# Sums of weight blocks in one ring with all other pieces, and one fixed PSUM tile for the product banks

## The chip, the cores and the metric

The kernel runs on one core of a Trainium2 chip. The metric is device time in microseconds. The kernel before took 2430.69 us, the median of three runs (2430.39 to 2430.94).

## What is computed

A trunk of two layers over 256 positions of width 2048, all in float32. Layer 0 mixes positions with a bidirectional mLSTM of 8 heads, layer 1 with a bidirectional HGRN2 of 16 heads; after each mixer comes a gated MLP of inner width 5504 with a convolution of width 3. Cut to the parts that the change touches, which are the matrix products with large weights:

```python
h = h + mixer(rmsnorm(h, g), w_in, ...) @ w_out          # w_out 2048 x 2048

u = rmsnorm(h, g2) @ w_up                                # w_up 2048 x 11008
a, v = jnp.split(u, 2, axis=-1)
c = conv_b + sum(ap[:, j:j + s] * conv_w[j] for j in range(3))
h = h + (jax.nn.gelu(c, approximate=False) * v) @ w_down # w_down 5504 x 2048
...
return rmsnorm(h, final_g)
```

## The kernel before

*Products in three matmuls.* TensorE multiplies in a float32 form of reduced precision, so every weight block and every activation is split in two parts, high and low (`wh`, `wl`; `xh`, `xl`), and a product is xh wh + xh wl + xl wh. ScalarE makes the high part (a cast), VectorE the low part (a subtraction). Weights pass through this once each: SP loads them in pieces of up to 1 MB into `raw` (three places), and `parts` splits them 1024 columns at a time into `wh` and `wl`, four places each.

*Chunks.* The kernel is a list of chunks, run one after the other by `stream`: "fm" (outputs by feature, the up-projection, q, k and gates), "tm" (outputs by token) and "st". `stream` takes split pieces from the generator `split_weights`, `LOOK` = 3 pieces ahead of their use. Every other job (norms, heads, sums of activations, the preparation below) is a generator in `side`, advanced by `tick`.

*The st chunks* are pairs of output columns computed by `squares_by_seven`. The 256 positions are two halves of 128, a pair of output blocks is two of 512 columns, and the inner dimension goes in units of two blocks of 128 rows. A plain unit needs eight products. Units named in `SEVEN` (for the MLP) or `SEVEN_MIX` (for the mixers' output) are done in seven, in Winograd's manner, with sums of activation blocks S1 to S4 and sums of weight blocks T1 to T4. A unit's weights lie in memory as B11, B22, B21, B12. The products P1, P5, P6, P7 collect in four PSUM banks of the pool `psm` (tag `mm`, two places of two banks, also used by the fm and tm chunks in turn), C11 to C22 in the four banks of `psa`. When the last unit by seven is done, `mid` reads P1, P5, P6, P7 into the output; after the last unit `done` adds C11 to C22.

In the MLP each part of the inner dimension (22 blocks, then 21) first runs its up-projection chunks. During these, `prepare` forms T1 to T4 of the coming units and writes them to memory (`tscr`). The first part then has two st chunks (d0 and d1, 11 units each, eight of them by seven), the second part has one st chunk (d0, 11 units, six by seven) and two tm chunks. In the mixers' output product there is one st chunk of 8 units, three by seven, whose T1 to T4 `weight_sums` forms on the spot.

*Where sums of weights live.* For a unit by seven, `combine` (L199 to L211) loads T1 to T4 as two tiles `T` of 1024 columns (tag `avc`, three places in the MLP, shared with the up-projection's evacuations `avc` of `done_up`, L1132 to L1143; two places in the mixers) or forms them, and splits them (L208, L209) into `th0`, `tl0`, `th1`, `tl1`, of which there is one place each. This is done for unit u+1 before unit u's first piece is split, or with `late` (mixers) after it. The two pieces of weights of unit u go through `wh`, `wl`; the sums are handed over with the second.

*Order.* Each engine runs its instructions in an order that was fixed at build time from a simulated timeline: an instruction goes in when its inputs and a place for its output are there, the ones that stand earlier in the program first. `pin` and `late(dst, src)` keep program order.

Of the kernel before, what the change touches and what calls it, by code (L numbers as in the profile page):

```python
# [8 lines left out]
F32 = mybir.dt.float32  # L9
# [33 lines left out]
RAW = 3  # L43
WB = 4
MIX = 5
LEAD = 48
TEMP = 3
GATES = 4 * AH
SEVEN = (1, 2, 3, 5, 6, 7, 8, 9), (1, 2, 4, 5, 7, 8)
SCRATCH = 4096  # L50
# [9 lines left out]
def trunk_kernel(ctx, tc, xT, x_d, fg_d, pp_d, cst_d, w_gate, w_first, w_aq, w_ak, w_av, w_ao, w_aout, w_ao2,  # L60
# [6 lines left out]
    ev = ctx.enter_context(tc.tile_pool(name="ev", bufs=1))  # L67
    psm = ctx.enter_context(tc.tile_pool(name="psm", bufs=2, space=PSUM))
    psa = ctx.enter_context(tc.tile_pool(name="psa", bufs=4, space=PSUM))
# [53 lines left out]

    pin = tc.keep_in_program_order

    def load_raw(src, b0, b1, start=nc.sync.dma_start):
# [4 lines left out]
    def split_weights(chunks):  # L131

        def parts(r, m, pin=lambda ins: ins):
            wh = wpool.tile([P, 1024], F32R, tag="wh", bufs=WB, name="wh")
            wl = wpool.tile([P, 1024], F32R, tag="wl", bufs=WB, name="wl")
            pin(act.copy(wh[:, :m], r))  # L136
            pin(dve.tensor_tensor(wl[:, :m], r, wh[:, :m].bitcast(F32), ALU.subtract))  # L137
            return wh, wl

        first, loaded = chunks[0], []  # L140
        raws = first.load(loaded, chunks[1])
        for k in range(KT):
            if k == 0:
                first.x(0, pin)
            wh, wl = parts(raws[k], 512, pin)
            if k:
                first.x(k, pin)
            yield wh, wl, 1
        for ch in chunks[1:]:
            if ch.kind == "st":  # L150
                yield from split_squares(ch, parts)
                continue
            total = ch.nk * ch.width
            for b0 in range(0, total, 2048):
                b1 = min(total, b0 + 2048)
                raw = loaded.pop(0) if loaded else load_raw(ch.src, b0, b1, late if ch.paced else nc.sync.dma_start)
                for c0 in range(0, b1 - b0, 1024):
                    m = min(1024, b1 - b0 - c0)
                    at = b0 + c0 if ch is chunks[1] else total
                    if at == 0:  # L160
                        first.gate()
                    if at < LOOK * 1024:
                        wh, wl = parts(raw[:, c0:c0 + m], m, pin)
                    elif ch is chunks[2] and b0 == c0 == 0:
                        wh, wl = parts(raw[:, c0:c0 + m], m, first.behind_v)
                    else:
                        wh, wl = parts(raw[:, c0:c0 + m], m)
                    if at == (LOOK - 1) * 1024:
                        first.sums()
                    yield wh, wl, m // ch.width  # L170

    def temporary(pool_, name):
        return pool_.tile([P, 1024], F32, tag="avc", bufs=TEMP if pool_.name == "ff" else 2, name=name)

    def weight_sums(a, b, T, T_):

        B22, B21, B12 = a[:, 512:1024], b[:, 0:512], b[:, 512:1024]
        dve.tensor_tensor(T.rearrange("p (a b) -> p a b", a=2), B12.unsqueeze(1).broadcast_to([P, 2, 512]),
                          a.rearrange("p (a b) -> p a b", a=2), ALU.subtract)
        yield 2.5  # L180
        dve.tensor_tensor(T_[:, 0:512], B22, T[:, 0:512], ALU.subtract)
        yield 2.5
        dve.tensor_tensor(T_[:, 512:1024], B21, T_[:, 0:512], ALU.subtract)

    def split_squares(ch, parts):

        units, raws, kept, sums = (ch.nk + 1) // 2, {}, {}, {}
        side.until(lambda: ch.waits is None or ch.waits)

        def raw(u):  # L190
            if u not in raws and u < units:
                raws[u] = load_raw(ch.src, 2048 * u, min(2048 * (u + 1), 1024 * ch.nk) - (512 if u in ch.stored else 0))
                if u in ch.stored:
                    kept[u] = [temporary(ch.pool, "T") for _ in range(2)]
                    for i, t in enumerate(kept[u]):
                        nc.sync.dma_start(t, ch.stored[u][:, i * 1024:(i + 1) * 1024])
            return raws.get(u)

        def combine(u):  # L199
            r = raw(u)  # L200
            T, T_ = kept[u] if u in kept else (temporary(ch.pool, "T") for _ in range(2))
            if u not in kept:
                for _ in weight_sums(r[:, 0:1024], r[:, 1024:2048], T, T_):
                    pass
            sums[u] = []
            for i, t in enumerate((T, T_)):
                th, tl = (ch.pool.tile([P, 1024], F32R, tag=n, name=n) for n in (f"th{i}", f"tl{i}"))
                act.copy(th, t)  # L208
                dve.tensor_tensor(tl, t, th.bitcast(F32), ALU.subtract)  # L209
                sums[u].append((th, tl))  # L210

        for u in range(units):
            r = raw(u)
            if u + 1 in ch.seven and not ch.late:
                combine(u + 1)
            wh, wl = parts(r[:, 0:1024], 1024)
            yield wh, wl, 1
            if u + 1 in ch.seven and ch.late:
                combine(u + 1)
            if 2 * u + 1 < ch.nk:  # L220
                m = 512 if u in ch.seven else 1024
                wh, wl = parts(r[:, 1024:1024 + m], m)
                yield wh, wl, sums.pop(u, None)

    def banks():
        return psm.tile([P, 2, 512], F32, tag="mm", name="mm")

    def squares_by_seven(ch, fetch, ready):
# [19 lines left out]
        for u in range(units):  # L248
# [3 lines left out]
            if 2 * u + 1 == ch.nk:  # L252
# [4 lines left out]
                break  # L257
            fetch()
            q = ready.pop(0)
            x0, x1 = ch.x(2 * u), ch.x(2 * u + 1)  # L260
            A11, A21, A12, A22 = half(x0, 0), half(x0, 1), half(x1, 0), half(x1, 1)
            B11, B22, B21 = block(p[:2], 0), block(p[:2], 1), block(q[:2], 0)
            if u in ch.seven:
                (S1, S3, S2, S4), t = ch.sums(u), q[2]
                T1, T3, T2, T4 = (block(t[i // 2], i % 2) for i in ((3, 1, 0, 2) if u in ch.stored else range(4)))
                for i, (ps, x, w) in enumerate(((P1, A11, B11), (C12, S4, B22), (C11, A12, B21), (P5, S1, T1),
                                                (P7, S3, T3), (P6, S2, T2), (C21, A22, T4))):
                    product(ps, x, w, u == last and ps in psm_)
                    side.tick(0.65)
                if u == last:  # L270
                    ch.mid(psm_)
                continue
            B12 = block(q[:2], 1)
            for ps, (x, w), (y, v) in ((C11, (A11, B11), (A12, B21)), (C12, (A11, B12), (A12, B22)),
# [78 lines left out]

    def fm_sum(ps, dst):
        b = ev.tile([P, T], F32, tag="b", bufs=3, name="b")
        act.copy(b, ps[:, T:2 * T])
        dve.tensor_tensor(dst, ps[:, 0:T], b, ALU.add)

    def fm_scaled(ps, R, dst, scale=None):
        fm_sum(ps, dst)  # L360
        if scale is None:
# [179 lines left out]

    def pair(src, nk, c0, x, sums, norm, seven, late=False):

# [29 lines left out]
        ch = Chunk("st", src, nk, x, done)  # L573
        ch.mid, ch.seven, ch.sums, ch.late = mid, seven, sums, late
        ch.stored, ch.waits = {}, None
        return ch

    def prepare(mp, todo, period, finished):
# [3 lines left out]
        def load(i):  # L582
            if i < len(todo):
                n = ("th", "tl")[i % 2]
                r = [mp.tile([P, 1024], F32, tag=f"{n}{j}", name=f"p{n}") for j in range(2)]
                for j in range(2):
# [16 lines left out]
    def mixed(w, w2, x, norm, close):  # L603
# [7 lines left out]

        two = pair(w2, KT, 1, x, sums, norm, SEVEN_MIX, True)

# [21 lines left out]
    def mlstm(norm, nxt):  # L635
# [114 lines left out]
        def two_parts(ps, name, scale=None):  # L750
            z = box["mp"].tile([P, T], F32, tag="qk", bufs=2, name="qk")
            zs = box["mp"].tile([P, 2 * T], F32R, tag=name, bufs=2, name=name)
            fm_scaled(ps, norm.R, z, scale)
            act.copy(zs[:, 0:T], z)
# [73 lines left out]
        for pr in range(AH // 2):  # L828
# [36 lines left out]
            def done_first(ps, done_v=done_v):  # L865
                pq = aux("pq")
                for k in range(KT):
                    o = k % 4 * GATES
                    pin(pe.matmul(pq[o:o + GATES, 0:T], gw[:, k], hx[:, k], start=k < 4, stop=k >= KT - 4))
                gs = ev.tile([P, T], F32, tag="b", bufs=3, name="gs")  # L870
                act.copy(gs, pq[:, 0:T])
# [40 lines left out]
    def hgrn(norm, nxt):  # L912
# [33 lines left out]
        def take(hd, what, ps):  # L946
            mp = box["mp"]
            st = heads[hd]
            if what == 0:
                st["q"] = mp.tile([P, T], F32, tag="q", bufs=2, name="q")  # L950
                fm_scaled(ps, norm.R, st["q"], box["oml"][:, hd:hd + 1])
                st["QK"] = mp.tile([P, 1152], F32, tag="QK", bufs=2, name="QK")
# [5 lines left out]
            z = mp.tile([P, T], F32, tag="z", bufs=2, name="z")  # L958
            fm_scaled(ps, norm.R, z)
            g = G[:, dr * T:(dr + 1) * T]  # L960
# [352 lines left out]
```

## Time and profile before

| | us, unless named |
|---|---|
| median of three runs | 2430.69 |
| the profiled execution | 2427.93 |
| its span | 2426.2 |
| moved by DMA | 578.14 MB, mean 238 GB/s |

The core's TensorE clock was 0.997 of full speed over the span. "PE" is TensorE's matmuls, "PEld" its weight loads, which overlap them; "DVE" is VectorE, "ACT" ScalarE, "POOL" GpSimd, "SP" the queue that issues nearly all loads. L238 is line 238 of the kernel, the matmul in `product` of `squares_by_seven`. A row of a stretch names its start and end in us from the span's start, its length, each engine's busy time with its count, the granted TensorE clock, the mean busy share of the 16 DMA engines and GB/s. A row of waits reads: engine, what it was about to do, what it waited for, us in total, times, longest. A row of a group reads: line, engine, operation, output and inputs, shapes, count, then busy us, mean ns of one, then the idle time before them and what ended it. The matmuls are pipelined, so that one shows 0.39 us though the next starts 0.23 us after it.

### The profile page before, as it was taken

To read this page: it belongs to the slowest core of one execution; us is meant where nothing else is said; L and a number is where in the kernel's file an instruction comes from. 1 tells how busy PE (TensorE), PEld (TensorE's weight loads), DVE (VectorE), ACT (ScalarE), POOL (GpSimd) and SP (SyncE) were. 2 spreads that over 40 slices of the span, in tenths; PEclk is the share of its full clock that TensorE was granted. 3 is DMA by queue.
4 is the path that set the end of the run, shared out by engine and by line. 5 is a ranking of instruction groups with operands and counts; after the bars stand their busy time and mean duration, and the time that the engine had idled before them with its cause. 6 is when DMAs were issued, how large, how long until landed. Compare 5 with 4: busy or idle time off the path is not lost.

```text
span 2426.2 us, 38067 instructions
## 1 busy us (share of the span) xinstructions
PE 2386.3 (98%) x14596; PEld 2030.4 (84%) x14596; DVE 1933.8 (80%) x3075; ACT 1349.0 (56%) x2055; POOL 194.2 (8%) x240
## 2 busy tenths in 40 slices
PE   9999999999999999999999999999999999999998
PEld 8888888888777888888888888887888877888886
DVE  7766687888778888777888888889798877888875
ACT  7655455555555555555555555556555555455553
POOL 0100000000000000001222232220000000000000
PEclk9999999999999999999999999999999999999999
DMA  8655556998887777755545554545898988777774
GB/s 308 188 180 174 174 191 231 332 332 308 318 305 265 270 241 243 267 193 192 175 159 172 167 172 167 173 158 191 282 340 325 329 305 301 246 250 243 249 269 147
DMA packets 105701, 578.14 MB, mean 238 GB/s; under 512 B 11936, under 2 KB 12448, under 8 KB 58672
## 3 DMA queue, kind: packets, MB, share of 16 engines
q1 hardware_dynamic: 103824, 571.71, 67.4%
q0 software_dynamic: 1120, 3.21, 0.8%
q8 instruction: 114, 1.87, 0.3%
q10 hardware_dynamic: 576, 0.79, 0.1%
q14 instruction: 67, 0.55, 0.1%
HBM read 527.37 MB, written 48.30 MB: 237 GB/s over the span
## 4 chain that ended last, share of the span: by engine, by line
PE 83%; DMA 7%; DVE 6%; issue 2%; ACT 1%; SPq 0%; POOL 0%; POOLq 0%; ACTq 0%; DVEq 0%
PE mm L329 31%; PE mm L345 21%; PE mm L333 16%; PE pc L238 7%; PE mm L238 4%; DVE wl L137 2%; DMA T<-tscr 2%; DMA pth<-in_w_d 2%; DMA ptl<-in_w_d 1%; DVE tl L209 1%; ACT th L208 1%; PE pn L792 1%; DMA raw<-in_w_d 1%; PE py L1050 1%; PE pd L1000 1%
## 5 line engine op out<-in xcount | busy, mean ns | idle before, releaser
L329 PE MATMUL mm<-xt,wh 128*128 128x512 f32 x3776 | 1315.0, 395 | 0.0
L137 DVE TENSOR_TENSOR wl<-raw,wh 128x1024 fp32r<-128x1024 f32 (+1 forms) x846 | 1005.6, 1196 | 303.9 <-ACT wh L136 302.5
L136 ACT CAST wh<-raw 128x1024 fp32r<-128x1024 f32 (+1 forms) x846 | 850.3, 1014 | 675.2 <-PE mm L329 403.8
L333 PE MATMUL mm<-xt,wl 128*128 128x256 f32 x3776 | 1049.2, 279 | 0.4 <-DVE wl L137 0.4
L329 PEld LDWEIGHTS mm<-xt,wh 128*128 128x128 f32 x3776 | 707.7, 188 | 160.3
L333 PEld LDWEIGHTS mm<-xt,wl 128*128 128x128 f32 x3776 | 711.0, 188 | 5.0 <-DVE wl L137 0.8
L345 PE MATMUL mm<-wh,xt 128*128 128x512 f32 x1024 | 322.7, 391 | 1.1 <-ACT xt L351 1.0
L345 PEld LDWEIGHTS mm<-wh,xt 128*128 128x128 f32 x1024 | 191.6, 188 | 40.8 <-ACT xt L351 1.5
L345 PE MATMUL mm<-wl,xt 128*128 128x512 f32 x512 | 200.2, 391 | 0.0
L209 DVE TENSOR_TENSOR tl<-T,th 128x1024 fp32r<-128x1024 f32 x100 | 120.1, 1221 | 60.8 <-ACT th L208 60.5
L238 PE MATMUL pc<-wh,g 128*128 128x512 f32 x488 | 163.3, 391 | 3.4 <-ACT wh L136 3.3
L208 ACT CAST th<-T 128x1024 fp32r<-128x1024 f32 x100 | 102.8, 1050 | 98.1 <-PE mm L238 56.3
L238 PE MATMUL mm<-th,sx 128*128 128x512 f32 x300 | 107.9, 397 | 10.6 <-ACT th L208 10.3
L238 PEld LDWEIGHTS pc<-wh,g 128*128 128x128 f32 x488 | 91.9, 188 | 24.1 <-ACT wh L136 5.1
L345 PEld LDWEIGHTS mm<-wl,xt 128*128 128x128 f32 x512 | 96.2, 188 | 18.9
L558 POOL TENSOR_TENSOR hm<-hm,u 128x512 f32<-128x512 f32 x8 | 12.4, 1546 | 1180.4 <-DVE u L557 1125.2
L345 PE MATMUL mm<-wh,g 128*128 128x512 f32 x308 | 96.3, 391 | 0.0
L238 PE MATMUL pc<-wl,g 128*128 128x512 f32 x244 | 95.6, 392 | 0.1
L1136 ACT ACTIVATE avc<-avc,pp 128x256 f32<-128x256 f32 x86 | 51.7, 601 | 51.4 <-DVE avc L1134 51.0
L238 PEld LDWEIGHTS mm<-th,sx 128*128 128x128 f32 x300 | 56.9, 190 | 26.3 <-ACT th L208 14.3
L597 DVE TENSOR_TENSOR ptl<-ptl 128x512 f32<-128x512 f32 x88 | 60.4, 686 | 23.2 <-DMA ptl<-in_w_d 22.9
L597 DVE TENSOR_TENSOR pth<-pth 128x512 f32<-128x512 f32 x88 | 60.3, 685 | 21.2 <-DMA pth<-in_w_d 15.0
(268 smaller groups left out, 2564.5 us busy)
## 6 DMA issues: line engine op xcount, KB each, us to landing
raw<-in_w_up SPq DMA_DIRECT2D x172, 1024.0 KB, 6.3
raw<-in_w_bq SPq DMA_DIRECT2D x48, 1024.0 KB, 5.0
T<-tscr SPq DMA_DIRECT2D x88, 512.0 KB, 5.5
raw<-in_w_d SPq DMA_DIRECT2D x40, 1024.0 KB, 5.2
raw<-in_w_d SPq DMA_DIRECT2D x44, 768.0 KB, 6.1
raw<-in_w_ao SPq DMA_DIRECT2D x24, 1024.0 KB, 4.8
pth<-in_w_d SPq DMA_DIRECT2D x44, 512.0 KB, 8.0
ptl<-in_w_d SPq DMA_DIRECT2D x44, 512.0 KB, 7.8
```

What stands on the lines that cost most here:

```text
L136: pin(act.copy(wh[:, :m], r))
L137: pin(dve.tensor_tensor(wl[:, :m], r, wh[:, :m].bitcast(F32), ALU.subtract))
L208: act.copy(th, t)
L209: dve.tensor_tensor(tl, t, th.bitcast(F32), ALU.subtract)
L238: pe.matmul(ps, a, b, start=id(ps) not in begun, stop=stop and i == 2)
L329: pe.matmul(ps[f], wh[:, c:c + P], x, start=k + kk == 0, stop=False)
L333: pe.matmul(ps[f][:, 0:T], wl[:, c:c + P], x[:, 0:T], start=False, stop=k + kk == ch.nk - 1)
L345: pe.matmul(ps[t], x[:, a + t * P:a + (t + 1) * P], w[:, c], start=st and i == 0, stop=sp and i == 2)
L597: dve.tensor_tensor(out, x, y, ALU.subtract)
L792: pe.matmul(pn[:, 0:258], w, v, start=(i == 0), stop=(i == len(parts) - 1))
L1000: pe.matmul(pd[o:o + QUAD, c:c + n], k[:, b * QUAD:(b + 1) * QUAD], q[:, t:t + n], start=True, stop=True)
L1136: act.activation(c, a, AF.Identity, bias=col("conv_b", layer * FT + f), scale=cw[1])
```

## The change

- `T` becomes one tile of 1536 columns that holds T2, T3, T4; T1 takes B12's place in `raw`. For stored units that is a load of 768 KB into `T` and one of 256 KB into the last quarter of `raw`, in place of two of 512 KB.
- `th` and `tl` go. A unit by seven now gives four pieces to `parts`: (B11, B22), (T2, T3), (B21, T1), (T4), each in order of use. In st chunks every third piece takes its place in the stage's own pool (tags `wh`, `wl` with `MORE` = 2 places) and the others in `wpool`'s four, so that there are six places in turn.
- For stored units `raw` and `T` are loaded when the unit itself comes; unit u+1 is no longer asked for ahead of unit u. For the mixers `combine` forms the sums of unit u+1 after the first piece of unit u, in four operations of 512 columns.
- The products are run in the order P1, C12, P6, P7, C11, P5, C21 (before: P1, C12, C11, P5, P7, P6, C21).
- The units by seven of the first part are 1 to 4 and 6 to 9 (before: 1 to 3 and 5 to 9).
- The four product banks are one tile, made once, whose halves `banks` hands out in turn.
- `prepare` uses the tags `wh`, `wl` of the stage's pool in place of `th`, `tl`. The buffer `b` of `fm_sum` moves from `ev` to the mixers' pools, and `gs` gets a place of its own.

```diff
-SEVEN = (1, 2, 3, 5, 6, 7, 8, 9), (1, 2, 4, 5, 7, 8)
+MORE = 2
+SEVEN = (1, 2, 3, 4, 6, 7, 8, 9), (1, 2, 4, 5, 7, 8)
...
+    four, turns = psm.tile([P, 4, 512], F32, name="mm"), dict(mm=0, w=0)
...
-        def parts(r, m, pin=lambda ins: ins):
-            wh = wpool.tile([P, 1024], F32R, tag="wh", bufs=WB, name="wh")
-            wl = wpool.tile([P, 1024], F32R, tag="wl", bufs=WB, name="wl")
+        def parts(r, m, pin=lambda ins: ins, more=None):
+            where, bufs = wpool, WB
+            if more is not None:
+                turns["w"] += 1
+                if turns["w"] % 3 == 0:
+                    where, bufs = more, MORE
+            wh, wl = (where.tile([P, 1024], F32R, tag=n, bufs=bufs, name=n) for n in ("wh", "wl"))
...
-        return pool_.tile([P, 1024], F32, tag="avc", bufs=TEMP if pool_.name == "ff" else 2, name=name)
+        return pool_.tile([P, 1536], F32, tag="avc", bufs=TEMP if pool_.name == "ff" else 2, name=name)
...
         def raw(u):
             if u not in raws and u < units:
-                raws[u] = load_raw(ch.src, 2048 * u, min(2048 * (u + 1), 1024 * ch.nk) - (512 if u in ch.stored else 0))
+                n = 1536 if u in ch.stored else min(2048, 1024 * ch.nk - 2048 * u)
+                raws[u] = load_raw(ch.src, 2048 * u, 2048 * u + n)
                 if u in ch.stored:
-                    kept[u] = [temporary(ch.pool, "T") for _ in range(2)]
-                    for i, t in enumerate(kept[u]):
-                        nc.sync.dma_start(t, ch.stored[u][:, i * 1024:(i + 1) * 1024])
+                    kept[u] = temporary(ch.pool, "T")
+                    nc.sync.dma_start(kept[u], ch.stored[u][:, 0:1536])
+                    nc.sync.dma_start(raws[u][:, 1536:2048], ch.stored[u][:, 1536:2048])
             return raws.get(u)
...
         def combine(u):
-            r = raw(u)
-            T, T_ = kept[u] if u in kept else (temporary(ch.pool, "T") for _ in range(2))
-            if u not in kept:
-                for _ in weight_sums(r[:, 0:1024], r[:, 1024:2048], T, T_):
-                    pass
-            sums[u] = []
-            for i, t in enumerate((T, T_)):
-                th, tl = (ch.pool.tile([P, 1024], F32R, tag=n, name=n) for n in (f"th{i}", f"tl{i}"))
-                act.copy(th, t)
-                dve.tensor_tensor(tl, t, th.bitcast(F32), ALU.subtract)
-                sums[u].append((th, tl))
+            r, T = raw(u), temporary(ch.pool, "T")
+            B11, B22, B21, B12 = (r[:, j * 512:(j + 1) * 512] for j in range(4))
+            T2, T3, T4 = (T[:, j * 512:(j + 1) * 512] for j in range(3))
+            for x, y, out in ((B12, B22, T3), (B12, B11, B12), (B22, B12, T2), (B21, T2, T4)):
+                dve.tensor_tensor(out, x, y, ALU.subtract)
+            kept[u] = T
...
         for u in range(units):
             r = raw(u)
-            if u + 1 in ch.seven and not ch.late:
+            yield *parts(r[:, 0:1024], 1024, more=ch.pool), 1
+            if u + 1 in ch.seven and u + 1 not in ch.stored:
                 combine(u + 1)
-            wh, wl = parts(r[:, 0:1024], 1024)
-            yield wh, wl, 1
-            if u + 1 in ch.seven and ch.late:
-                combine(u + 1)
+            if u in ch.seven:
+                yield *parts(kept[u][:, 0:1024], 1024, more=ch.pool), 1
             if 2 * u + 1 < ch.nk:
-                m = 512 if u in ch.seven else 1024
-                wh, wl = parts(r[:, 1024:1024 + m], m)
-                yield wh, wl, sums.pop(u, None)
+                yield *parts(r[:, 1024:2048], 1024, more=ch.pool), 1
+            if u in ch.seven:
+                yield *parts(kept[u][:, 1024:1536], 512, more=ch.pool), 1
...
     def banks():
-        return psm.tile([P, 2, 512], F32, tag="mm", name="mm")
+        turns["mm"] = 2 - turns["mm"]
+        return four[:, turns["mm"]:turns["mm"] + 2]
...
+            def products(*them):
+                for ps, x, w in them:
                     product(ps, x, w, u == last and ps in psm_)
                     side.tick(0.65)
+
+            def piece():
+                fetch()
+                q = ready.pop(0)[:2]
+                return block(q, 0), block(q, 1)
+
+            B11, B22 = block(p[:2], 0), block(p[:2], 1)
             if u in ch.seven:
-                (S1, S3, S2, S4), t = ch.sums(u), q[2]
-                T1, T3, T2, T4 = (block(t[i // 2], i % 2) for i in ((3, 1, 0, 2) if u in ch.stored else range(4)))
-                for i, (ps, x, w) in enumerate(((P1, A11, B11), (C12, S4, B22), (C11, A12, B21), (P5, S1, T1),
-                                                (P7, S3, T3), (P6, S2, T2), (C21, A22, T4))):
-                    product(ps, x, w, u == last and ps in psm_)
-                    side.tick(0.65)
+                S1, S3, S2, S4 = ch.sums(u)
+                products((P1, A11, B11), (C12, S4, B22))
+                T2, T3 = piece()
+                products((P6, S2, T2), (P7, S3, T3))
+                B21, T1 = piece()
+                products((C11, A12, B21), (P5, S1, T1))
+                T4, _ = piece()
+                products((C21, A22, T4))
                 if u == last:
                     ch.mid(psm_)
                 continue
...
-    def fm_sum(ps, dst):
-        b = ev.tile([P, T], F32, tag="b", bufs=3, name="b")
+    def fm_sum(mp, ps, dst):
+        b = mp.tile([P, T], F32, tag="b", bufs=3, name="b")
...
-                n = ("th", "tl")[i % 2]
-                r = [mp.tile([P, 1024], F32, tag=f"{n}{j}", name=f"p{n}") for j in range(2)]
+                n = ("wh", "wl")[i % 2]
+                r = [mp.tile([P, 1024], F32, tag=n, bufs=MORE, name=f"p{n}") for _ in range(2)]
...
-                gs = ev.tile([P, T], F32, tag="b", bufs=3, name="gs")
+                gs = ev.tile([P, T], F32, tag="gs", name="gs")
```

More of the change, by code (lines that the diff above doesn't have):

```diff
@@ L67, in trunk_kernel @@
     ev = ctx.enter_context(tc.tile_pool(name="ev", bufs=1))
-    psm = ctx.enter_context(tc.tile_pool(name="psm", bufs=2, space=PSUM))
+    psm = ctx.enter_context(tc.tile_pool(name="psm", bufs=1, space=PSUM))
     psa = ctx.enter_context(tc.tile_pool(name="psa", bufs=4, space=PSUM))
@@ L172, in temporary @@
     def temporary(pool_, name):
-        return pool_.tile([P, 1024], F32, tag="avc", bufs=TEMP if pool_.name == "ff" else 2, name=name)
[L175 to L183, printed above, removed]
+        return pool_.tile([P, 1536], F32, tag="avc", bufs=TEMP if pool_.name == "ff" else 2, name=name)
     def split_squares(ch, parts):
-        units, raws, kept, sums = (ch.nk + 1) // 2, {}, {}, {}
+        units, raws, kept = (ch.nk + 1) // 2, {}, {}
         side.until(lambda: ch.waits is None or ch.waits)
@@ L257, in squares_by_seven @@
                 break
-            fetch()
-            q = ready.pop(0)
             x0, x1 = ch.x(2 * u), ch.x(2 * u + 1)
             A11, A21, A12, A22 = half(x0, 0), half(x0, 1), half(x1, 0), half(x1, 1)
-            B11, B22, B21 = block(p[:2], 0), block(p[:2], 1), block(q[:2], 0)
-            if u in ch.seven:
-                (S1, S3, S2, S4), t = ch.sums(u), q[2]
-                T1, T3, T2, T4 = (block(t[i // 2], i % 2) for i in ((3, 1, 0, 2) if u in ch.stored else range(4)))
-                for i, (ps, x, w) in enumerate(((P1, A11, B11), (C12, S4, B22), (C11, A12, B21), (P5, S1, T1),
-                                                (P7, S3, T3), (P6, S2, T2), (C21, A22, T4))):
+            def products(*them):
+                for ps, x, w in them:
                     product(ps, x, w, u == last and ps in psm_)
                     side.tick(0.65)
+            def piece():
[3 more added lines that the diff above has]
+            B11, B22 = block(p[:2], 0), block(p[:2], 1)
+            if u in ch.seven:
+                S1, S3, S2, S4 = ch.sums(u)
[6 more added lines that the diff above has]
+                products((C21, A22, T4))
                 if u == last:
@@ L272, in squares_by_seven @@
                 continue
-            B12 = block(q[:2], 1)
+            B21, B12 = piece()
             for ps, (x, w), (y, v) in ((C11, (A11, B11), (A12, B21)), (C12, (A11, B12), (A12, B22)),
@@ L352, in split, with fm_scaled @@
         pin(dve.scalar_tensor_tensor(dst[:, T:2 * T], src, gcol, dst[:, 0:T].bitcast(F32), ALU.mult, ALU.subtract))
-    def fm_sum(ps, dst):
-        b = ev.tile([P, T], F32, tag="b", bufs=3, name="b")
+    def fm_sum(mp, ps, dst):
+        b = mp.tile([P, T], F32, tag="b", bufs=3, name="b")
         act.copy(b, ps[:, T:2 * T])
         dve.tensor_tensor(dst, ps[:, 0:T], b, ALU.add)
-    def fm_scaled(ps, R, dst, scale=None):
-        fm_sum(ps, dst)
+    def fm_scaled(mp, ps, R, dst, scale=None):
+        fm_sum(mp, ps, dst)
         if scale is None:
@@ L540, in token_sums, with pair @@
         return [(sx[:, i * P:(i + 1) * P], sx[:, m + i * P:m + (i + 1) * P]) for i in range(m // P)] + ([last] if last else [])
-    def pair(src, nk, c0, x, sums, norm, seven, late=False):
+    def pair(src, nk, c0, x, sums, norm, seven):
         def part(t, c):
@@ L573, in pair @@
         ch = Chunk("st", src, nk, x, done)
-        ch.mid, ch.seven, ch.sums, ch.late = mid, seven, sums, late
-        ch.stored, ch.waits = {}, None
+        ch.mid, ch.seven, ch.sums = mid, seven, sums
+        ch.stored, ch.waits, ch.pool = {}, None, None
         return ch
@@ L610, in sums @@
             return SX[u]
-        two = pair(w2, KT, 1, x, sums, norm, SEVEN_MIX, True)
+        two = pair(w2, KT, 1, x, sums, norm, SEVEN_MIX)
         def token():
@@ L752, in two_parts @@
             zs = box["mp"].tile([P, 2 * T], F32R, tag=name, bufs=2, name=name)
-            fm_scaled(ps, norm.R, z, scale)
+            fm_scaled(box["mp"], ps, norm.R, z, scale)
             act.copy(zs[:, 0:T], z)
@@ L950, in take @@
                 st["q"] = mp.tile([P, T], F32, tag="q", bufs=2, name="q")
-                fm_scaled(ps, norm.R, st["q"], box["oml"][:, hd:hd + 1])
+                fm_scaled(mp, ps, norm.R, st["q"], box["oml"][:, hd:hd + 1])
                 st["QK"] = mp.tile([P, 1152], F32, tag="QK", bufs=2, name="QK")
@@ L958, in take @@
             z = mp.tile([P, T], F32, tag="z", bufs=2, name="z")
-            fm_scaled(ps, norm.R, z)
+            fm_scaled(mp, ps, norm.R, z)
             g = G[:, dr * T:(dr + 1) * T]
```

## The prediction

> **What bounds the kernel now.** I read the page first, then the busy time of stretches, then who waits for whom inside them.
>
> ```profile
> span 2426.2 us, 38067 instructions
> PE 2386.3 (98%) x14596; PEld 2030.4 (84%) x14596; DVE 1933.8 (80%) x3075; ACT 1349.0 (56%) x2055; POOL 194.2 (8%) x240
> ```
>
> TensorE is busy 98% of the span, so nothing that leaves its matmuls as they are can save much more than its idle 40 us and what it loses in pace. The change touches only the stretches of line 238, the products of `squares_by_seven`. Their matmuls by stretch (us, PE busy and count, PEld, clock, DMA share, GB/s):
>
> ```profile
> 636.50:762.00 125.50, 116.41 (x480) 89.73 (x480) 0.99 0.83 298
> 994.80:1048.00 53.20, 53.19 (x234) 43.77 (x234) 1.00 0.75 269
> 1947.50:2073.50 126.00, 115.28 (x480) 89.99 (x480) 0.99 0.82 293
> 2306.40:2359.60 53.20, 53.20 (x234) 43.73 (x234) 1.00 0.76 275
> ```
>
> The second row gives TensorE's pace when nothing holds it: 53.2 / 234 = 0.2273 us per matmul; the fourth runs at the same. The first and third are the double pairs at the first part of each FFN (d0 and d1, 22 blocks of rows each, 480 matmuls): 480 x 0.2273 = 109.1 us, so they lose 16.4 and 16.9 us. The last stretch with line 238 is the middle of the second mixer's output product; here all engines' rows (PE, PEld, DVE, ACT, POOL) are needed:
>
> ```profile
> 1630.70:1677.20 46.50, 44.52 (x192) 34.93 (x190) 41.07 (x60) 24.52 (x31) 0.00 (x0) 1.00 0.50 173
> 323.90:365.40 41.50, 41.50 (x185) 34.37 (x184) 38.71 (x57) 23.09 (x29) 0.00 (x0) 1.00 0.59 205
> ```
>
> 192 x 0.2273 = 43.6, so 2.9 us are lost there, and nothing in the first mixer's (185 in 41.5 us). **All that the change can win is 16.4 + 16.9 + 2.9 = 36.2 us.**
>
> What is late in the first double pair, for PE and for SP's queue, and who is behind it:
>
> ```profile
> PE mm L238 <- ACT th L208: 4.8, 5, 1.8
> PE mm L238 <- DVE tl L209: 1.5, 2, 0.8
> PE mm L238 <- DVE u L557: 0.3, 1, 0.3
> ...
> SPq L196 <- DVE tl L209: 53.3, 28, 5.8
> ...
> ACT th L208 <- PE mm L238: 15.8, 9, 5.6
> ACT th L208 <- DMA T<-tscr: 7.7, 5, 2.5
> ```
>
> PE waits for the split parts of the sums (`th`, `tl`). ScalarE cannot make them because it waits 15.8 us for PE to leave the only place of `th` and 7.7 us for the sums' load `T`; and SP held those loads back 53.3 us, 28 times, until VectorE had emptied a `T`. It is a loop with too few places: the split of unit u+1's sums waits for PE's products of unit u, the load of u+2's for that split. A late product costs more than its wait:
>
> ```profile
> 662.42 0.50 PE L238 MATMUL mm<-th,sx 128*128 128x512 f32 x1 [1.79 <-ACT th L208]
> 663.59 0.54 PE L238 MATMUL mm<-th,sx 128*128 128x512 f32 x1 [0.66 <-ACT th L208]
> 664.35 0.63 PE L238 MATMUL mm<-tl,sx 128*128 128x512 f32 x1
> ...
> 667.34 0.63 PE L238 MATMUL mm<-th,sx 128*128 128x512 f32 x2
> 667.80 0.40 PE L238 MATMUL mm<-tl,sx 128*128 128x512 f32 x1
> ```
>
> After two waits of 1.79 and 0.66 us the matmuls start 0.42 us apart until 667.3, some ten of them, 2 us more. The Trainium skill (TensorE: Matmul & The Clock Gate, section "Part 1: The HAM clock gate") has the clock halve only after an idle window of about 3.4 us; this trace halves the pace after 2.45 us in two pieces, so the measurement decides. By the page, stalls of 2 us that remain would cost only themselves.
>
> **The change part by part.** The work first. A unit by seven had, per engine, two 1024-wide splits of sums, one 1024-wide and one 512-wide of weights:
>
> ```profile
> L209 DVE TENSOR_TENSOR tl<-T,th 128x1024 fp32r<-128x1024 f32 x32 | 38.4, 1221 | 19.2 <-ACT th L208 19.2
> L208 ACT CAST th<-T 128x1024 fp32r<-128x1024 f32 x32 | 33.0, 1050 | 29.2 <-PE mm L238 15.8 <-DMA T<-tscr 7.7 <-issue 2.8
> L137 DVE TENSOR_TENSOR wl<-raw,wh 128x1024 fp32r<-128x1024 f32 x29 | 35.1, 1220 | 9.6 <-ACT wh L136 9.6
> L137 DVE TENSOR_TENSOR wl<-raw,wh 128x512 fp32r<-128x512 f32 x16 | 11.8, 735 | 0.0
> L136 ACT CAST wh<-raw 128x512 fp32r<-128x512 f32 x16 | 9.8, 615 | 0.0
> ```
>
> After the change it has pieces of 1024 (B11, B22), 1024 (T2, T3), 1024 (B21, T1) and 512 (T4): the same four splits, 3 x 1.22 + 0.74 = 4.40 us on VectorE and 3 x 1.05 + 0.62 = 3.77 us on ScalarE, against 21 x 0.2273 = 4.77 us of PE. Matmuls: 8 units by seven of 11 before and after, so 480 again; PE's work changes by 0. Loads: three per unit before (768 + 512 + 512 KB) and after (768 + 768 + 256 KB), the same 1792 KB; SP's issues too.
>
> *The ring.* Six places (four, and two in the stage's own pool), used in order: piece j+6 can be split once PE has done piece j. In a row of units by seven T4 of unit u reuses the place of T2, T3 of unit u-1, which PE leaves 4 x 0.682 = 2.7 us into that unit (0.682 = three matmuls). So T4(u) is split some 4 us into unit u-1, its `T` (one place of three, no longer two) is free then, and the load of unit u+3 is issued 0.8 us before unit u begins. With 6.1 us (768 KB row below) it lands 5.3 us after. The place of T2, T3 of u+3 comes free only when PE has left T4 of u+1, at 9.5 us: **the load has 4.2 us to spare**, where now it is the last to arrive. If a stall empties the ring, T4 is split three pieces (3.7 us) after its load lands; with the load 9.8 us for three units, against 14.3 us of PE: it recovers. So I count the stalls in the steady rows at 0.
>
> ```profile
> raw<-in_w_d SPq DMA_DIRECT2D x44, 768.0 KB, 6.1
> ...
> 621.73 0.33 SPq L128 DMA_DIRECT2D raw<-in_w_d  x1
> 635.88 0.32 SPq L196 DMA_DIRECT2D T<-tscr  x1
> 639.76 3.77 SPq L196 DMA_DIRECT2D T<-tscr  x2
> ```
>
> *The start of a double pair* stays exposed: `T` shares its three places with the up-projection's blocks, and the first came free at 635.88, the next at 639.76 and 643.2. Unit 1 begins at 636.5 + 24 x 0.2273 = 641.96 and takes T2, T3 two products later, at 643.3. Its load lands at 635.9 + 6.1 = 642.0, split by 643.05 and 644.3: 0.7 us late. If the last block takes the second place, T(2) is issued at 643.2, lands at 649.3 and is split by 651.6, and is wanted at 642.7 + 4.8 + 1.4 + 0.2 = 649.0: 2.6 late. While ScalarE's copy waits for that load, B21 and T4 of the unit and that block's own steps stand behind it; PE needs them later, and that block's PSUM banks at unit 1. Bounds 0.7, and 0.7 + 2.6 plus the 2 us of slow pace = 5.3; I take 3.0, the middle.
>
> *P6 comes three products earlier, P7 one* (third and fourth instead of sixth and fifth): 2.0 and 0.7 us. In the second pair they stand behind VectorE's reads of the first pair's (the 0.3 us row, L557 reads P7): 0.3 + 0.7 = 1.0 for P7, and between 0 and 2.0 for P6, which is read before P7. I take 1.2 in all.
>
> Each double pair thus loses 4.2 in place of 16.4 and 16.9: gains 12.2 and 12.7.
>
> *The mixers.* `combine` becomes four 512-wide operations instead of one of 1024 and two of 512 (rows of 0.69 and 1.22 us below): + 0.15 us, six times, hidden by VectorE's idle 2.8 us in the first mixer (38.71 of 41.5) and 5.4 in the second; without that cover 0.9. `combine` now always follows the first piece, as it did here. In the second mixer PE waits:
>
> ```profile
> L178 DVE TENSOR_TENSOR T<-raw 128x1024 f32<-128x1024 f32 x3 | 3.7, 1221 | 3.2 <-PE pz L1071 3.2
> L183 DVE TENSOR_TENSOR T<-raw,T 128x512 f32<-128x512 f32 x3 | 2.1, 688 | 0.0
> ...
> PE mm L238 <- DVE tl L209: 1.1, 1, 1.1
> ```
>
> The 1.1 goes, since T4 has a piece of its own, half as wide, and is used last. Bounds -0.9 and 2.9; I take 1.1.
>
> *One PSUM tile.* The banks turn as before; in the waits quoted PE waits for a bank to be read out only in the 0.3 us. 0. *`b` and `gs` in other pools, `T` wider*: places only; 0.
>
> **Sum:** 12.2 + 12.7 + 1.1 = 26.0. The profiled execution took 2427.93 us (span 2426.2), so 2401.9; the median lies 2.8 above it: **2404.7, say 2405.** With the bounds of the terms (losses of 0.7 to 5.3 + 2.0 in each double pair, so gains of 9.1 to 15.7 and 9.6 to 16.2, and -0.9 to 2.9 in the mixer: 17.8 to 34.8 in all), 2396 to 2413.
>
> **Rivals.** *Transfers bind* (14%). Four units by seven in a row now stand twice in each pair, and need 1.835 MB per 4.77 us, 385 GB/s.
>
> ```profile
> 650.00:660.00 10.00, 10.00 (x45) 8.27 (x45) 8.80 (x12) 5.99 (x8) 0.00 (x0) 1.00 0.95 312
> 740.00:750.00 10.00, 9.02 (x40) 7.17 (x39) 7.86 (x8) 6.82 (x8) 0.00 (x0) 1.00 1.01 409
> ```
>
> For it: 312 GB/s at 0.95 of the DMA engines' time. Against: 409 in the second row, and the mean need is 2 x 17.83 MB in 109.1 us, 327. At 312 a row of four takes 23.5 us instead of 19.1; two units loaded ahead cover about 3.5, so 1 us is lost in each of eight rows: 8 us less gain, 2413. The Trainium skill (DMA: Bandwidth & Descriptors, section "Specifications") gives HBM per core about 358 GB/s, which speaks against such rows too; at 358 a row lasts 20.5 us and the two units ahead cover it. The 409 over 10 us is above the page's figure.
>
> *Slower: the sums come late everywhere* (13%). For stored units the load stood in the program a unit or more ahead; now it stands with its own unit, three pieces ahead. If SP issues it only then, T2, T3 of a unit that follows one by seven have 4.8 us for 6.1 + 1.05 + 1.2 less the 0.2 of the first matmul: 3.4 late; after a whole unit 7.5 us: 0.7 late. First parts: (6 x 3.4 + 2 x 0.7) x 4 pairs = 87; second parts, which lose nothing now, (3 x 3.4 + 3 x 0.7) x 2 = 25; less the 33.3 lost now: +79, 2509. It decides as soon as the load waits for its turn in the program instead of a free place. Against: the pair's first raw was issued at 621.73, 14.8 us before its first product, where three of an up block's four pieces are 8.3 us (232.8 / 21 blocks = 11.1 us, row below): SP runs ahead of the program as soon as a place is free, and the 53.3 us of SP's waits were all for places.
>
> ```profile
> 762.00:994.80 232.80, 232.80 (x1344) 203.74 (x1344) 190.10 (x272) 126.80 (x178) 4.64 (x2) 1.00 0.73 246
> ```
>
> *Slower: banks of one tile wait for each other* (5%). Then every up block's first matmul waits for the block before to be read out:
>
> ```profile
> L1133 DVE TENSOR_TENSOR avc<-mm,avc 128x512 f32<-128x512 f32 x86 | 58.8, 683 | 1.4 <-ACT avc L1132 1.4
> L1132 ACT COPY avc<-mm 128x512 f32<-128x512 f32 x86 | 49.7, 578 | 1.7 <-DVE g L1143 1.7
> ```
>
> 86 x 1.26 = 108, 2536 at least. Against: elsewhere parts of a tile are followed apart, as `gx`, read from 4.3 us on while parts of it are still sent for until 14.5:
>
> ```profile
> L351 ACT ACTIVATE xt<-gx x16: 502/505/508, 4.3 to 24.2; 128x256 fp32r<-128x256 f32 x16
> L661 SPq DMA_DIRECT2D gx<-in_xT x7: 328/328/443, 1.6 to 14.5; - x7
> ```
>
> *It moves the stalls* (8%): `T` held until its last piece keeps the last up block, and so its banks, from being read out, and unit 1 waits as long as PE waits now. No change, 2430.
>
> **How the numbers follow.** The forecast has 60%. Its own range is 2396 to 2413; with no change and the bound transfers 82% lie between 2394, where all 36 us go, and 2434. I tell no change as within 0.2% (4.9 us), about what a measurement here can tell. Faster: 60 + 14 + 2 of the last rival = 76%; the same 5%; slower 13 + 5 + 1 = 19%.
>
> **What would show it.** After: the two stretches of 480 matmuls take 112 to 115 us each, PE's waits there sum to some 2 to 4 us, all at units 1 and 2; SP's waits for `T` end well before PE needs it; no slow pace in the middle. It is wrong if PE waits for `wh` or `wl` fed from `T` in each unit by seven, if the stretches of 234 and 183 grow, or if matmuls of up blocks begin to wait for `avc`.

## The result, and the profile after

The changed kernel takes 3090.94 us (median of four runs, 3086.17 to 3101.65) against 2430.54: 1.2724 times as long, 95% interval 1.269 to 1.2757. The forecast of 2405 has the wrong sign. The page of the profile after, its first lines and its row of the clock:

```profile
span 3089.2 us, 37917 instructions
PE 2685.5 (87%) x14596; PEld 2248.3 (73%) x14596; DVE 1977.0 (64%) x3081; ACT 1370.2 (44%) x2055; POOL 158.3 (5%) x240
...
PEclk9999998787899888899999999999878899987899
```

The span is 663 us longer. TensorE does the same 14596 matmuls, is idle 3089.2 - 2685.5 = 403.7 us instead of 39.9, and busy 299 us longer for the same work. The clock row says how: it was granted only 0.7 to 0.9 in several slices. Whom TensorE waits for, over the whole span:

```profile
PE mm L332 <- DVE avc L1136: 235.5, 82, 3.1
PE mm L332 <- DVE q L360: 27.9, 8, 3.5
PE mm L348 <- DVE qk L360: 14.1, 4, 3.5
PE mm L332 <- DVE qk L360: 13.8, 4, 3.5
...
PE mm L332 <- DVE Vl L839: 11.5, 4, 3.6
```

L332 and L348 are the matmuls of the fm and tm chunks. L1136 is the addition with which the *last up block* is read out of its banks, L360 reads out q, k and the gates, L839 v. None of these rows is there before the change. The next chunk writes other banks than those, and still waits. Where that stands in the stages (us, then busy time of PE, PEld, DVE, ACT and POOL, clock, DMA share, GB/s), first after the change, then before it without the stage from 762.00, whose row the prediction has:

```profile
5.50:409.20 403.70, 348.66 (x1642) 288.88 (x1643) 228.03 (x411) 193.33 (x320) 17.53 (x31) 0.92 0.48 160
478.40:848.90 370.50, 310.02 (x1419) 263.86 (x1420) 227.36 (x338) 139.95 (x199) 0.70 (x1) 0.81 0.62 220
960.00:1303.90 343.90, 286.82 (x1347) 242.55 (x1348) 194.94 (x270) 129.85 (x178) 3.54 (x2) 0.84 0.49 170
1356.40:2064.10 707.70, 616.88 (x4954) 515.34 (x4953) 487.32 (x957) 322.01 (x593) 112.86 (x179) 0.95 0.42 141
2137.20:2507.80 370.60, 310.17 (x1418) 263.90 (x1419) 226.66 (x338) 139.12 (x199) 0.70 (x1) 0.81 0.61 217
2620.50:2965.20 344.70, 287.15 (x1344) 244.27 (x1345) 191.78 (x268) 129.34 (x177) 4.74 (x6) 0.83 0.50 172
```

```profile
5.40:323.90 318.50, 317.35 (x1643) 268.30 (x1644) 223.41 (x407) 190.92 (x320) 16.49 (x31) 1.00 0.60 202
390.00:636.50 246.50, 246.05 (x1422) 215.10 (x1421) 211.70 (x331) 135.53 (x195) 0.70 (x1) 1.00 0.88 320
1047.90:1630.60 582.70, 576.57 (x4955) 495.26 (x4953) 481.81 (x958) 317.42 (x593) 145.60 (x179) 1.00 0.51 172
1702.00:1947.50 245.50, 245.50 (x1421) 214.70 (x1420) 214.81 (x335) 137.68 (x197) 0.70 (x1) 1.00 0.90 323
2073.50:2306.40 232.90, 232.90 (x1346) 203.56 (x1345) 190.84 (x272) 126.86 (x178) 5.75 (x6) 1.00 0.74 249
```

| stage | before, us | after, us | more |
|---|---|---|---|
| four up-projections (86 blocks) | 957.7 | 1429.7 | +472.0 |
| first mixer | 318.5 | 403.7 | +85.2 |
| second mixer | 582.7 | 707.7 | +125.0 |
| two double pairs | 251.5 | 220.5 | -31.0 |

These make 651 of the 663 us. Each up block takes 5.5 us more. Half of that is idle time and half is pace: summed over the four stages, PE is idle for 235 us that were not there before, and busy 237 us longer. One boundary between two blocks, PE's timeline after the change, then ScalarE's and VectorE's over the same time:

```profile
575.47 0.39 PE L332 MATMUL mm<-xt,wh 128*128 128x512 f32 x1
575.70 0.27 PE L336 MATMUL mm<-xt,wl 128*128 128x256 f32 x1
578.85 0.80 PE L332 MATMUL mm<-xt,wh 128*128 128x512 f32 x1 [2.88 <-DVE avc L1136]
579.45 0.42 PE L336 MATMUL mm<-xt,wl 128*128 128x256 f32 x1
579.66 0.63 PE L332 MATMUL mm<-xt,wh 128*128 128x512 f32 x1
580.09 0.41 PE L336 MATMUL mm<-xt,wl 128*128 128x256 f32 x1
580.30 0.63 PE L332 MATMUL mm<-xt,wh 128*128 128x512 f32 x1
```

```profile
575.90 1.04 ACT L142 CAST wh<-raw 128x1024 fp32r<-128x1024 f32 x1 [1.72 <-PE mm L332]
576.85 0.58 ACT L1135 COPY avc<-mm 128x512 f32<-128x512 f32 x1
...
576.97 1.23 DVE L143 TENSOR_TENSOR wl<-raw,wh 128x1024 fp32r<-128x1024 f32 x1 [0.94 <-ACT wh L142]
578.12 0.68 DVE L1136 TENSOR_TENSOR avc<-mm,avc 128x512 f32<-128x512 f32 x1
```

The last matmul of the block ends at 575.97. ScalarE's copy out of the banks stands behind a cast (1.04 us), VectorE's addition behind a subtraction (1.23 us); it ends at 578.80, and 0.05 us later PE begins the next block. Then a pair of matmuls takes 0.64 us where it took 0.35 (575.12 to 575.47). In the block before this one the slow pace lasted from 561.80 to 567.7: nine pairs in 5.9 us, which take 3.1 us at the full pace, so 2.8 us were lost. The rows of this time and of the rest of that block show the granted clock halved, 0.50, and then back at 0.99:

```profile
561.80:567.70 5.90, 5.90 (x18) 5.02 (x19) 2.06 (x4) 1.61 (x3) 0.00 (x0) 0.50 0.95 342
567.80:575.90 8.10, 8.10 (x47) 6.90 (x46) 6.37 (x8) 2.76 (x5) 0.00 (x0) 0.99 0.32 90
```

The other parts of the change made no such loss. The double pairs, line 230 now, in the changed kernel:

```profile
848.90:959.40 110.50, 109.60 (x480) 89.67 (x480) 1.00 0.83 302
2507.80:2617.80 110.00, 109.43 (x480) 89.77 (x480) 1.00 0.85 314
```

They took 125.5 and 126.0 before, and 480 matmuls take 109.1 at the pace of the stretches in which nothing holds them. Here they follow up blocks that were slowed; e1 below shows them without that.

### The profile page after: what moved, and what is told of

The parts are those of the page before. It is cut to its first block, busy times and chain, and to the rows that moved or that the text cites. A ratio compares the mean times of both kernels' runs of the same rounds, so it can differ in the third digit from the quotient of the medians.

```text
span 3089.2 us, 37917 instructions
## 1 busy us (share of the span) xinstructions
PE 2685.5 (87%) x14596; PEld 2248.3 (73%) x14596; DVE 1977.0 (64%) x3081; ACT 1370.2 (44%) x2055; POOL 158.3 (5%) x240
## 4 chain that ended last, share of the span: by engine, by line
PE 72%; DVE 11%; ACT 4%; issue 2%; DMA 0%; SPq 0%; POOLq 0%; POOL 0%; DVEq 0%; ACTq 0%
PE mm L332 31%; PE mm L336 15%; PE mm L348 13%; PE pc L230 7%; DVE wl L143 5%; PE mm L230 4%; ACT wh L142 3%; DVE avc L1136 2%; DVE kq L995 0%; DVE QK L1016 0%; PE py L1053 0%; DVE QK L1015 0%; PE pa L1003 0%; PE pz L409 0%; PE pd L1003 0%
## 5 line engine op out<-in xcount | busy, mean ns | idle before, releaser
L332 PE MATMUL mm<-xt,wh 128*128 128x512 f32 x3776 | 1568.9, 450 | 298.7 <-DVE avc L1136 235.5
L332 PEld LDWEIGHTS mm<-xt,wh 128*128 128x128 f32 x3776 | 826.6, 219 | 532.1 <-DVE avc L1136 261.6
L336 PE MATMUL mm<-xt,wl 128*128 128x256 f32 x3776 | 1159.6, 308 | 0.0
L336 PEld LDWEIGHTS mm<-xt,wl 128*128 128x128 f32 x3776 | 831.2, 220 | 4.0
L348 PE MATMUL mm<-wh,xt 128*128 128x512 f32 x1024 | 334.9, 403 | 24.7 <-DVE qk L360 14.1
L348 PEld LDWEIGHTS mm<-wh,xt 128*128 128x128 f32 x1024 | 197.7, 193 | 70.3 <-DVE qk L360 15.4
L348 PE MATMUL mm<-wl,xt 128*128 128x512 f32 x512 | 204.4, 400 | 0.0
L143 DVE TENSOR_TENSOR wl<-T,wh 128x1024 fp32r<-128x1024 f32 (+1 forms) x100 | 95.7, 960 | 30.1 <-ACT wh L142 29.5
L348 PEld LDWEIGHTS mm<-wl,xt 128*128 128x128 f32 x512 | 99.3, 194 | 19.9 <-issue 0.3
L142 ACT CAST wh<-T 128x1024 fp32r<-128x1024 f32 (+1 forms) x100 | 83.5, 837 | 55.4 <-PE pc L230 22.0
L230 PE MATMUL mm<-wh,sx 128*128 128x512 f32 x300 | 102.8, 389 | 0.0
L348 PE MATMUL mm<-wh,g 128*128 128x512 f32 x308 | 98.2, 396 | 2.6 <-ACT jk L503 2.3
L600 DVE TENSOR_TENSOR pwl<-pwl 128x512 f32<-128x512 f32 x88 | 60.5, 687 | 19.1 <-DMA pwl<-in_w_d 18.4
L1142 ACT ACTIVATE avc<-avc 128x256 f32<-128x256 f32 x86 | 35.8, 417 | 78.4 <-DVE avc L1141 78.4
L348 PEld LDWEIGHTS mm<-wh,g 128*128 128x128 f32 x308 | 58.5, 190 | 15.5 <-issue 3.2
```

The source lines that it names most:

```text
L230: pe.matmul(ps, a, b, start=id(ps) not in begun, stop=stop and i == 2)
L332: pe.matmul(ps[f], wh[:, c:c + P], x, start=k + kk == 0, stop=False)
L336: pe.matmul(ps[f][:, 0:T], wl[:, c:c + P], x[:, 0:T], start=False, stop=k + kk == ch.nk - 1)
L348: pe.matmul(ps[t], x[:, a + t * P:a + (t + 1) * P], w[:, c], start=st and i == 0, stop=sp and i == 2)
L600: dve.tensor_tensor(out, x, y, ALU.subtract)
L1142: act.activation(c, c, AF.Gelu)
```

## The experiments

Theory A: waits are kept per PSUM tile, so with one tile every chunk waits until the chunk before is read out; the ring itself works. Theory C: the ring is to blame, for instance because `T` keeps the places into which the up blocks are read out. Rival B: a tile that is made once and never given back is what does harm.

**e1: the PSUM part undone.**

```diff
-    psm = ctx.enter_context(tc.tile_pool(name="psm", bufs=1, space=PSUM))
+    psm = ctx.enter_context(tc.tile_pool(name="psm", bufs=2, space=PSUM))
...
-        turns["mm"] = 2 - turns["mm"]
-        return four[:, turns["mm"]:turns["mm"] + 2]
+        return psm.tile([P, 2, 512], F32, tag="mm", name="mm")
```

> The changed kernel with the PSUM banks given back to two places of two banks each (as before the change); the ring stays. Theory A (the one PSUM tile makes every chunk wait until the chunk before has been read out, the ring itself works): the 660 us go, and the ring's gain shows: the two double pairs at 110 to 113 us as in the changed kernel, so 2430.5 - 15 - 16 - 2 = 2397 to 2405 us. Theory C (the ring or the longer hold of the avc places delays the up blocks' read-out): stays near 3090.

2401.97 us (2399.37 to 2404.23; before 2429.3 in the same session), ratio 0.9881, interval 0.9851 to 0.9911. Theory C falls. The double pairs and their waits in e1:

```profile
637.50:750.40 112.90, 110.62 (x480) 89.34 (x480) 1.00 0.88 325
1938.50:2049.80 111.30, 110.76 (x480) 89.25 (x480) 1.00 0.88 327
```

```profile
PE mm L229 <- ACT wh L142: 1.3, 1, 1.3
PE pc L229 <- DVE wl L143: 0.8, 1, 0.8
PE mm L229 <- DVE wl L143: 0.2, 1, 0.2
```

Of the 8.8 us in which PE waited in the first double pair 2.3 are left, all within its first two units (the longest at 647.45).

**e2: the PSUM part alone, in the kernel before.**

```diff
-    psm = ctx.enter_context(tc.tile_pool(name="psm", bufs=2, space=PSUM))
+    psm = ctx.enter_context(tc.tile_pool(name="psm", bufs=1, space=PSUM))
...
+    four, turns = psm.tile([P, 4, 512], F32, name="mm"), dict(mm=0)
...
-        return psm.tile([P, 2, 512], F32, tag="mm", name="mm")
+        turns["mm"] = 2 - turns["mm"]
+        return four[:, turns["mm"]:turns["mm"] + 2]
```

> The kernel before with nothing changed but the PSUM banks: one tile of four banks, made once. Theory A: all of the loss and none of the ring's gain, 3091 + 33 = about 3120 us, with PE waiting some 235 us for the up blocks' read-out. Theory C: stays at 2430.

3140.52 us (3137.91 to 3143.13), ratio 1.2924 (1.2873 to 1.2975). The same waits with the old scheme of sums:

```profile
PE mm L331 <- DVE avc L1135: 236.5, 82, 3.5
PE mm L331 <- DVE q L359: 27.8, 8, 3.5
PE mm L240 <- ACT th L209: 15.0, 8, 2.5
```

This one edit makes the whole loss, and the third row, absent from the changed kernel, is the old loop of sums. It is 20 us more than expected. The double pairs take 129.6 and 130.7 us here, 8.8 us more than before the change in all; the rest of the 20 was not traced.

**e3: two tiles of two banks, each made once.**

```diff
-    four, turns = psm.tile([P, 4, 512], F32, name="mm"), dict(mm=0, w=0)
+    halves, turns = [psm.tile([P, 2, 512], F32, name=f"mm{i}") for i in range(2)], dict(mm=0, w=0)
...
-        turns["mm"] = 2 - turns["mm"]
-        return four[:, turns["mm"]:turns["mm"] + 2]
+        turns["mm"] = 1 - turns["mm"]
+        return halves[turns["mm"]]
```

> The changed kernel with two PSUM tiles of two banks, each made once and handed out in turn. Theory A (waits are kept per tile, so halves of one tile wait for each other): like e1, 2397 to 2405. Rival B (a tile that is made once and never released is what orders the chunks badly): stays near 3090.

2402.80 us, ratio 0.9889 (0.9864 to 0.9914), as e1. That a tile is made once and kept is harmless; that both halves are one tile is the cause. Rival B falls.

**e9: the one tile declared flat.**

```diff
-    four, turns = psm.tile([P, 4, 512], F32, name="mm"), dict(mm=0, w=0)
+    four, turns = psm.tile([P, 2048], F32, name="mm"), dict(mm=0, w=0)
...
-        return four[:, turns["mm"]:turns["mm"] + 2]
+        return four[:, 512 * turns["mm"]:512 * turns["mm"] + 1024].rearrange("p (a b) -> p a b", a=2)
```

> The changed kernel with its one PSUM tile declared flat, 128 x 2048, its halves cut out as column ranges, as gx is cut in memory. If waits are kept per PSUM tile whatever its shape: 3090 us again. If only the three-dimensional form hid that the halves lie apart: 2402.

3092.41 us (a single run), with 235.4 us of waits for the up blocks' read-out. The shape does not matter: as this kernel is built, a PSUM tile is followed as a whole, where `gx` in the other memory is followed by parts.

**e4: the array kept busy during the wait.** `ch.paced` is true for the up blocks and for no other chunk.

```diff
+            if ch.paced:
+                fill = aux("fill")
+                for _ in range(13):
+                    pe.matmul(fill, wh[:, 0:P], x, start=True, stop=True)
             ch.done(both if ch.paced else ps)
```

> The changed kernel with 13 matmuls of 512 columns more at the end of each of the 86 up blocks, into a spare bank and read by nobody (2.96 us of work in the wait of 3.1). Theory A says that of the 5.75 us that an up block loses 3.1 are the wait and 2.65 the halved clock after it: with the array kept busy the second part goes, 86 x 2.5 = 215 us less, about 2875 us, clock near 1.0 in the up stages. If the slow pace has another cause than the idle array, the time stays at 3090 or rises.

2913.11 us (2909.97 to 2916.24): 178 us less than the changed kernel with 1118 matmuls more. The same kind of boundary in e4, and then its first up stage:

```profile
545.36 0.28 PE L336 MATMUL mm<-xt,wl 128*128 128x256 f32 x1
545.47 3.17 PE L354 MATMUL fill<-xt,wh 128*128 128x512 f32 x13
548.48 0.39 PE L332 MATMUL mm<-xt,wh 128*128 128x512 f32 x1
548.71 0.28 PE L336 MATMUL mm<-xt,wl 128*128 128x256 f32 x1
548.82 0.40 PE L332 MATMUL mm<-xt,wh 128*128 128x512 f32 x1
```

```profile
475.40:791.80 316.40, 316.03 (x1704) 270.38 (x1705) 227.24 (x341) 141.00 (x201) 0.70 (x1) 1.00 0.73 257
```

The next block begins 3.0 us after the start of the fill, and at once at full pace (548.48 to 548.82, 0.34 us a pair); the clock is 1.00 where it was 0.81, and a block takes (791.8 - 475.4) / 22 = 14.4 us in place of 16.8. That the idle time brings the slow clock is thus shown. I had expected 215 us less. The four up stages, in order, win 54, 44, 53 and 23 us, 174 in all. In the first stage of 21 blocks a block wins 2.1 us ((343.9 - 300.3) / 21) and not 2.5, and in the last stage the fill itself waits for casts, 20.4 us in all, as in no other stage:

```profile
PE fill L354 <- ACT wh L142: 20.4, 20, 1.0
```

**e5: the units by seven as before, five in a row.** `SEVEN` is (1, 2, 3, 5, 6, 7, 8, 9) again, on top of e1.

> e1 (ring, two PSUM places) with the units by seven of the first part as before the change, 1 to 3 and 5 to 9, five in a row in place of four. Theory A (a load has some 4 us to spare in the ring, DMA does not bind): within 3 us of e1, 2399 to 2405. Rival (transfers bind in long rows of units by seven, 1 us and more in each): 2406 or more, with PE waiting in the middle of the double pairs.

2401.01 us, ratio 0.9884 (0.986 to 0.9908): no difference to e1. Its double pairs move 325 and 329 GB/s over 112 us, and PE does not wait in their middle.

**e6: a ring of four.** On top of e1, the two places in the stage's pool are left unused.

```diff
-                if turns["w"] % 3 == 0:
+                if turns["w"] < 0:
```

> e1 with the two places in the stage's own pool left unused: a ring of four. Theory A: T4 of unit u then reuses the place of its own B11, B22, so that it is split only some 2.5 us before it is wanted, and the load three units on has no longer 4 us but about 1 us to spare: the double pairs lose some of the gain, 2405 to 2420. If only the order of use counts and not the number of places, 2402.

2401.48 us, ratio 0.9885 (0.9861 to 0.9908). The double pairs:

```profile
635.80:747.50 111.70, 110.12 (x480) 89.59 (x480) 1.00 0.87 320
1936.20:2046.60 110.40, 109.86 (x480) 89.65 (x480) 1.00 0.87 320
```

I missed: two places fewer cost nothing that shows, so the gain does not come from having six. What brings it, the order of use or the single `T` for each unit, this run does not separate; e8 bears on that.

**e8: a fourth place for `T`, in the kernel before.** `TEMP` is 4 instead of 3, nothing else.

> The kernel before the change with four places for the sums' loads and the up blocks in place of three, nothing else. Theory A says that two places were short, that of th and tl and that of T: with T's alone mended, ScalarE's 7.7 us of waits for T shrink, its 15.8 us for th stay, and a third of the ring's 28 us may come: 2415 to 2428. If T alone was the cause, 2402 to 2408; if th alone, 2430.

2410.58 us (2406.16 to 2417.43), ratio 0.9923 (0.9896 to 0.9949). The double pairs take 117.2 and 118.7 us, so one place more for the loads (the up blocks share it) brings 15.6 of the 27.3 us that the ring brings there. What ScalarE waits for in the first of them:

```profile
ACT th L208 <- PE mm L238: 11.0, 7, 5.6
ACT wh L136 <- PE pc L238: 10.0, 5, 4.5
...
ACT th L208 <- DMA T<-tscr: 2.3, 1, 2.3
```

The wait for `T` fell from 7.7 to 2.3 us, that for the one place of `th` from 15.8 to 11.0. I had put a third of the gain on `T`, 2415 to 2428 us, and missed: it was more than half. What brings the other part is not shown by a run of its own.

**e11: the first two units of each pair plain.** On top of e1, `SEVEN` is (2, 3, 4, 5, 6, 7, 8, 9).

> e1 with the units by seven of the first part moved to 2 to 9, so that the first two units of each pair are plain (eight in a row then follow). If what the double pairs still lose in e1 (113.0 and 111.3 us against 109.1) is the first sums' load, which waits for a place that the up blocks hold, the extra 5.4 us of plain unit cover it: 109.5 to 111 us each, 2398 to 2400. If transfers bind in long rows, eight in a row cost 0.7 us each beyond what is loaded ahead: 113 us and more, 2403 or more.

2400.5 us, ratio 0.99 (0.9875 to 0.9924), double pairs 111.9 and 112.1 us. Between the two expectations, and no better than e1: the first pair gained 1 us and the second lost 0.8. That the first load is what e1's double pairs still lose is not shown.

## Why the prediction was wrong

*The step that failed* is the one on one PSUM tile: "The banks turn as before [...] 0." I put nothing there because in the waits that I quoted PE waited only 0.3 us for a bank, and because `gx` is followed by parts. The first says only that two tiles are enough; the second is about a tile outside PSUM, and does not hold for this one inside it. What the runs show in place of the 0 is a loss of 660 us and more; PE's waits for the read-out of the up blocks are 235.5 us of it. The right mechanism stood among the rivals with 5%: banks of one tile wait for each other. So did its sign, the last one of the prediction: matmuls of up blocks wait for `avc`. e2 (alone, 3140.5), e3 (two tiles, 2402.8) and e9 (flat, 3092.4) leave none of the other causes named here.

*The rival's own size* was short as well: 86 x 1.26 us "at least" is 108 us, the up stages grew by 472. Three things were missing. The two operations that read a block out stand behind a cast and a subtraction, so that 1.26 became 2.87 (235.5 / 82). The wait halves the clock after it, some 2.8 us more, which e4 takes away. And the mixers grow by 210 us: PE is idle 139 us more in them (145.9 in place of 7.3) and busy 72 us longer. On the clock the trace has waits of 2.88 us and then 5.9 us at half pace; the Trainium skill (TensorE: Matmul & The Clock Gate, section "Part 1: The HAM clock gate") asks for an idle window of about 3.4 us before the clock falls. By that these waits would have cost themselves alone; here they cost nearly double.

*The ring* was right in sum, in part by luck: 12.2 and 12.7 us predicted for the double pairs, 125.5 - 112.9 = 12.6 and 126.0 - 111.3 = 14.7 measured in e1, whose 2402 us is 3 below the 2405 forecast for the whole. The pairs gained 2.4 us more than the sum had for them and the second mixer 2.8 us less, which nearly cancels. Its single terms:

- The steady rows at 0: nearly right. In the first pair PE waits only at the first two units; in the second it waits 0.4 us in all. My reason, that six places give 4.2 us to spare, is not needed: four do (e6).
- The start of a double pair at 3.0 us: e1 loses 3.8 and 2.2 against 109.1 in all, of which PE's waits are 2.3 in the first.
- P6 and P7 earlier, 1.2 us: 0. PE's waits in e1 have no row for that read any more.
- Transfers: they don't bind. e1 moves 325 and 327 GB/s through whole double pairs, e5 with five units in a row 325 and 329.
- The sums late everywhere, 2509 us: did not happen. The stretches of 234 matmuls take some 53 us in e1, as before.
- The second mixer, + 1.1: wrong in sign. It takes 48.2 us in e1 in place of 46.5. T1 now lies where B12 was, so the piece (B21, T1) of weights cannot be cast before VectorE has made it; the waits of that stretch in e1:

```profile
ACT wh L142 <- DVE raw L201: 3.7, 2, 2.7
...
PE pc L229 <- ACT wh L142: 2.8, 4, 1.7
```

VectorE makes two units' sums at once here, after a queue of sums of activations; the cast begins at 1646.00, and PE waits 1.7 us for it. Before the change that piece needed only the load.

## What to carry to other kernels

Ask of every tile that is merged or split how far waits are told apart inside it: two halves that are used in turn must be two PSUM tiles here, even if the addresses stay the same. When a wait at a boundary is priced, add the work that stands ahead of the releasing operations on their engines, and the slow clock afterwards. Where a row of splits starves, look first whether loads wait for a place (one more place of `T` brought over half the gain here) before counting places of the split parts.

## What was not expected of the hardware

Idle times of only 2.9 us, one every 17 us, halve the matmul pace for some 6 us after each: the mean clock of the up stages was 0.81 to 0.84. Thirteen useless matmuls in each gap brought it to 1.00, and the kernel ran 178 us faster with more work.
